# One block product fewer in each pair of layer A's projections, and attention operands read from two halves in turn

## The chip, the cores and the metric

The kernel runs on one core of a Trainium2 chip. The metric is the device time of one execution in microseconds (us), the median of three runs. A profile of one more execution shows where the time lies. TensorE is called PE here (its weight loads PEld), VectorE DVE, ScalarE ACT, GpSimd POOL, and SyncE, which issues most of the transfers, SP.

## What is computed

Two layers of a sequence model on 256 positions of width 2048, in float32. Layer A projects the normalised input to queries, keys, values and gates (4096 wide each, 32 heads of 128), attends in chunks with a learned bias by relative distance, multiplies by a gate and projects back to 2048. Layer B does the same with shared keys and values, a forget gate and a causal mask.

```python
# layer A
h = rms_norm(x, a_norm)
q, k, v, g = split(h @ a_w_in, 4)              # 2048 -> 4 x 4096
o = chunked_relbias_attention(q, k, v, a_rel_bias)
x = x + (o * silu(g)) @ a_w_out                # 4096 -> 2048
# layer B
k, v = split(rms_norm(x, kv_norm) @ kv_w, 2)
logf = log_sigmoid(rms_norm(x, kv_norm) @ f_w + f_b)
q, g = split(rms_norm(x, b_norm) @ b_w_in, 2)
o = forgetting_attention(q, k, v, cumsum(logf))
x = x + (o * silu(g)) @ b_w_out
return rms_norm(x, final_norm)
```

## The kernel before

**Products in three parts.** Float32 accuracy comes from splitting each operand into a high and a low part (`hi` by an ACT copy that rounds, `lo` by a DVE subtraction) and adding three products: hi times hi, hi times lo, lo times hi. `mm3` does this for the projections, `dot3` for the attention and the block products. The activations, split once, are the stationary operands (`xT`, `oA`, `x1T`, `oB`); the weights stream past.

**Units and sub-blocks.** A projection is cut into units of 512 output columns. A unit holds two accumulators of 128 positions by 512 columns (`acc[0]`, `acc[1]`) in PSUM. Layer A's input projection has 32 units: for each of the 16 head pairs g one for queries and keys (`aqk`) and one for values and gates (`avg`). A unit takes 8 sub-blocks; a sub-block is 256 rows of the weights (2 blocks of 128, 512 KB). It costs 12 matmuls of 128x512: 2 blocks, 2 halves of the positions, 3 parts.

**The feed.** `Feed` loads the sub-blocks on SP's queue in the order of one list, into 6 buffers (`raw`), and splits each into one of 4 buffers `hi` and `lo`. `get` hands the oldest to PE and splits ahead: while PE works on one sub-block, the third behind it is split, as soon as the buffer that PE has just left is free. The weights lie in two halves of each row (`IL` = 2), and `cols` reads them as the moving operand in turn, one element from the first half, one from the second, 2 KB apart.

**Attention beside it.** Each head pair's attention is a generator (`attention`, called by `side_a` and `side_b`) which is advanced between sub-blocks by tables (`PV_STEPS`, `QK_STEPS`, `OLD_A_STEPS`): a transposition of q and k (`turn`: one DVE pass, then 16 transfers, in layer A 12 issued by POOL and 4 by ACT), the split of k (`wideh`, `widel`) and q, the scores (`s1p`, `s0p`, in banks of the 4-bank pool `ps_at`), the softmax, a transposition of the probabilities (`sg`; 16 transfers by POOL), their split, the product with the values (`op`) and the gate (`oT`, `oA`). So the work of one pair lies beside the projections of the next. The scores and `op` take their moving operands, 256 positions, in one contiguous run.

**Block products.** In the output projections (`ao`, `bo`) some sub-blocks of two units are computed together by `Quad`: 2 halves of the positions, 2 blocks of rows and 2 units make a 2x2 by 2x2 product, done with 7 products of blocks where 8 would be plain: 21 matmuls of 128x512, not 24. DVE forms sums of the weights (`Quad.split`: four subtractions beside the splits), sums of the activations (`Quads.open`), and adds the partial results p1, p5, p7, p6, which fill all 4 banks of `ps_at`, into `comb` (one ACT copy, four DVE additions). The first quad's sub-blocks of both units come as two `raw` tiles, `one` and `two`; `Quad.split` subtracts the two halves of `two` ahead of anything else that it does.

**Order.** Each engine runs its instructions in the order in which they stand in its queue, and an instruction that waits holds all behind it. The order follows the code, where a scheduler may move an instruction that waits for nothing far ahead; `tc.issue_after(x)` keeps what is written under it behind instruction x.

## Time and profile before

| | |
|---|---|
| runs | 1755.29 us median (1753.59 to 1757.29) |
| profiled execution | 1757.04 us, its span 1755.3 us |
| granted PE clock | 0.998 |
| PE busy | 1738.7 us (99%), 8348 matmuls |
| DVE busy | 1243.2 us (71%) |
| ACT busy | 1107.2 us (63%) |
| POOL busy | 516.6 us (29%) |
| DMA | 396.35 MB, 226 GB/s |

The span runs from the first instruction of the profiled execution to the last; 1.7 us of the time lie around it. A row of the timeline gives start, duration, engine, line, operation and tiles; a square bracket at its end gives the idle time before it and what ended it. A row of a group gives after its shapes the count, then the busy time in us and the mean of one in ns, then idle time before. A PE row's duration is the whole passage of a matmul, about 380 ns, and matmuls overlap, so the cost of one is read from the distance of the starts. The table of windows gives the length of a window, then the busy time of each engine (instructions in brackets), the clock, the DMA engines' share and GB/s. Layer A's input projections take the span to about 710 us, `ao` to 873, layer B's projections to 1580, `bo` the rest. Names of engines with a q at the end (SPq) are their queues of transfers.

### The profile page before, as it was taken

How to read it: one execution, taken by the hardware profiler on the slowest of the kernel's cores; microseconds unless marked ns; L12 is line 12 of the kernel's file. 1: busy time of each engine (PE TensorE's matmuls, PEld its weight loads, DVE VectorE, ACT ScalarE, POOL GpSimd, SP SyncE). 2: the span in 40 equal slices, each digit the busy share in tenths (PEclk: the TensorE clock that was granted, in tenths of full speed). 3: DMA queues.
4: the chain of work that ended last, by engine and by line, in shares of the span. 5: the costliest groups of instructions: out<-in, count | busy, mean ns of one | idle time of the engine just before them, and what ended most of it. 6: DMA issues, size and time to landing. Idle time of an engine off the chain costs nothing.

```text
span 1755.3 us, 25640 instructions
## 1 busy us (share of the span) xinstructions
PE 1738.7 (99%) x8348; PEld 1527.7 (87%) x8348; DVE 1243.2 (71%) x1818; ACT 1107.2 (63%) x2103; POOL 516.6 (29%) x1071
## 2 busy tenths in 40 slices
PE   9999999999999999999999999999999999999997
PEld 7888888888888888888888888888888888888886
DVE  7666666666666686688966777777777777876687
ACT  6555555555555566556657777777777777665454
POOL 2333333333333333202103333333333333333000
PEclk9999999999999999999999999999999999999999
DMA  8776776776777677677767777777767777767654
GB/s 301 241 222 222 227 225 223 226 224 225 224 222 226 224 224 230 202 241 250 245 214 234 226 226 224 224 227 225 224 226 225 225 226 225 245 214 233 218 203 144
DMA packets 143654, 396.35 MB, mean 226 GB/s; under 512 B 31104, under 2 KB 38560, under 8 KB 143392
## 3 DMA queue, kind: packets, MB, share of 16 engines
q1 hardware_dynamic: 107472, 354.25, 62.9%
q0 software_dynamic: 32256, 37.29, 6.5%
q10 hardware_dynamic: 3792, 3.17, 0.6%
q8 instruction: 66, 1.08, 0.3%
q14 instruction: 68, 0.56, 0.1%
HBM read 351.05 MB, written 4.23 MB: 202 GB/s over the span
## 4 chain that ended last, share of the span: by engine, by line
PE 96%; DMA 1%; DVE 1%; ACT 0%; issue 0%; SPq 0%; POOL 0%; DVEq 0%; ACTq 0%
PE bkv_acc L184 19%; PE bqg_acc L184 19%; PE avg_acc L184 18%; PE aqk_acc L184 18%; PE bo_acc L184 8%; PE ao_acc L184 7%; PE op L575 1%; PE s0p L541 1%; PE p L519 0%; PE p L517 0%; PE p L518 0%; PE op L518 0%; PE s1p L518 0%; PE s1p L519 0%; PE s1p L517 0%; PE op L519 0%
## 5 line engine op out<-in xcount | busy, mean ns | idle before, releaser
L490 POOL DMA_DIRECT2D sgZ<-sgY x512 | 251.0, 497 | 193.8 <-DVE sgY L487 90.6
L490 POOL DMA_DIRECT2D turned<-turned x448 | 219.9, 498 | 265.3 <-PE avg_acc L184 94.7
L243 DVE SCALAR_TENSOR_TENSOR bqg_lo<-bqg_raw,gain,bqg_hi 128x512 fp32r<-128x512 f32 x256 | 182.6, 750 | 84.4 <-ACT bqg_hi L242 84.2
L242 ACT ACTIVATE bqg_hi<-bqg_raw,gain 128x512 fp32r<-128x512 f32 x256 | 170.7, 714 | 107.4 <-PE bqg_acc L184 51.8
L248 DVE TENSOR_TENSOR avg_lo<-avg_raw,avg_hi 128x1024 fp32r<-128x1024 f32 x127 | 153.3, 1219 | 109.6 <-ACT avg_hi L247 107.9
L248 DVE TENSOR_TENSOR aqk_lo<-aqk_raw,aqk_hi 128x1024 fp32r<-128x1024 f32 x125 | 152.4, 1219 | 86.8 <-ACT aqk_hi L247 85.4
L247 ACT ACTIVATE avg_hi<-avg_raw 128x1024 fp32r<-128x1024 f32 x127 | 132.4, 1055 | 121.2 <-PE aqk_acc L184 68.6
L243 DVE SCALAR_TENSOR_TENSOR bkv_lo<-bkv_raw,gain,bkv_hi 128x512 fp32r<-128x512 f32 x256 | 181.0, 748 | 38.3 <-ACT bkv_hi L242 35.6
L184 PE MATMUL bqg_acc<-bqg_hi,x1Th 128*128 128x512 f32 x512 | 192.2, 386 | 0.0
L184 PE MATMUL aqk_acc<-aqk_hi,xTh 128*128 128x512 f32 x512 | 190.4, 382 | 1.5 <-ACT aqk_hi L247 1.5
L184 PE MATMUL aqk_acc<-aqk_lo,xTh 128*128 128x512 f32 x512 | 189.1, 380 | 1.2 <-DVE aqk_lo L248 1.2
L184 PE MATMUL avg_acc<-avg_hi,xTh 128*128 128x512 f32 x512 | 190.2, 382 | 0.0
L184 PE MATMUL bqg_acc<-bqg_lo,x1Th 128*128 128x512 f32 x512 | 189.6, 381 | 0.0
L184 PE MATMUL bqg_acc<-bqg_hi,x1Tl 128*128 128x512 f32 x512 | 189.4, 380 | 0.0
L184 PE MATMUL bkv_acc<-bkv_hi,x1Th 128*128 128x512 f32 x512 | 189.1, 380 | 0.0
L247 ACT ACTIVATE aqk_hi<-aqk_raw 128x1024 fp32r<-128x1024 f32 x125 | 131.5, 1052 | 91.2 <-PE aqk_acc L184 43.5
L184 PE MATMUL bkv_acc<-bkv_lo,x1Th 128*128 128x512 f32 x512 | 188.9, 379 | 0.0
L184 PE MATMUL avg_acc<-avg_lo,xTh 128*128 128x512 f32 x512 | 188.9, 379 | 0.0
L184 PE MATMUL avg_acc<-avg_hi,xTl 128*128 128x512 f32 x512 | 188.9, 379 | 0.0
L184 PE MATMUL bkv_acc<-bkv_hi,x1Tl 128*128 128x512 f32 x512 | 188.9, 379 | 0.0
L184 PE MATMUL aqk_acc<-aqk_hi,xTl 128*128 128x512 f32 x512 | 188.9, 379 | 0.0
L242 ACT ACTIVATE bkv_hi<-bkv_raw,gain 128x512 fp32r<-128x512 f32 x256 | 168.7, 712 | 22.9 <-PE bqg_acc L184 16.5
(297 smaller groups left out, 3556.0 us busy)
## 6 DMA issues: line engine op xcount, KB each, us to landing
bqg_raw<-in_b_w_in SPq DMA_DIRECT2D x128, 512.0 KB, 4.3
bkv_raw<-in_kv_w SPq DMA_DIRECT2D x128, 512.0 KB, 4.0
avg_raw<-in_a_w_in SPq DMA_DIRECT2D x127, 512.0 KB, 4.2
aqk_raw<-in_a_w_in SPq DMA_DIRECT2D x125, 512.0 KB, 3.9
ao_raw<-in_a_w_out SPq DMA_DIRECT2D x64, 512.0 KB, 4.4
bo_raw<-in_b_w_out SPq DMA_DIRECT2D x64, 512.0 KB, 4.1
sgZ<-sgY POOLq DMA_DIRECT2D x512, 40.0 KB, 4.0
turned<-turned POOLq DMA_DIRECT2D x448, 32.0 KB, 3.7
```

The source lines that it names most:

```text
L184: pe.matmul(acc[t], x[:, t * P:(t + 1) * P], w, start=t not in begun, stop=last and i == 2)
L242: act.activation(hi[:, :, j], raw[:, :, j], AF.Copy, scale=gk)
L243: dve.scalar_tensor_tensor(lo[:, :, j], raw[:, :, j], gk, r32(hi[:, :, j]), op0=OP.mult, op1=OP.subtract)
L247: self.by_act = act.activation(hi[:, :, j], raw[:, :, j], AF.Copy)
L248: self.by_dve = dve.tensor_sub(lo[:, :, j], raw[:, :, j], r32(hi[:, :, j]))
L490: queues[j].dma_start(out=r32(z)[j * SQ:(j + 1) * SQ, i], in_=y[i * SQ:(i + 1) * SQ, j])
L541: pe.matmul(s0p[:, i], q0[:, i], qkT[:, HG + i, 0], start=True, stop=True)
L575: pe.matmul(op[:, i, P:], v1[:, i * DH:(i + 1) * DH], pT[:, i, NT], start=False, stop=i == HG - 1)
```

## The change

1. **A quad in each pair of layer A.** For g from 1 to 15, the last sub-block of `aqk` and that of `avg` (b = 7) become one quad, `a_pairs[g - 1]`. It is fed and run behind the fifth sub-block of the pair's first unit (`QUAD_STEP` = 5). It is a quad by itself, first and last, so its four products are combined at once into `comb`, an SBUF tile of its own. The query and key part of `comb` is scaled by ACT and added in the read-out of `aqk`, which moves from two ACT copies to two DVE operations; the value and gate part is added in `close_vg` by two DVE additions, and what follows reads SBUF and not PSUM. The activations' sums are formed once (`sum_up` after the first pair).
2. **Attention's steps** move to fit (`FIRST_STEPS`, `SECOND_STEPS`, `OLD_A_STEPS`): a pair's scores now stand behind the first sub-block of the next pair, the transposition of the probabilities behind the third, `op` behind the fourth sub-block of the next pair's second unit; the last pair's steps beside `ao` follow suit.
3. **Operands read in turn.** `split_pairs` writes hi and lo of an operand into one tile with its two halves of positions 2 KB apart, and the scores, `op` and the forget gate's `zp` read one position from each half in turn. The results come out interleaved, and the readers of `s1p`, `op` and `zp` in PSUM step over two elements; the two last products of `op` write every second column.
4. **Sums queued.** The sums in `Quads.open` are put behind the newest split on DVE (`tc.issue_after`).
5. The buffers of the first transposition (`home`) and of the start are laid into other tiles.

The diff, without the tile layout of the start:

```diff
-QK_STEPS = {0: 1, 6: 1, 7: 2}
-PV_STEPS = {1: 1}
-OLD_A_STEPS = {0: 1, 2: 99}
+QUAD_STEP = 5
+SECOND_STEPS = {0: 1, 6: 1}
+FIRST_STEPS = {0: 2, 2: 1}
+OLD_A_STEPS = {1: 1, 3: 99}
...
+                with tc.issue_after(feed.by_dve.ins):
+                    self.sum_up(lhs, b, two[:, b % 2], free)
...
+        def sum_up(self, lhs, b, dst, free):
+            self.sums[b] = dst
+            hi, lo = dst[:, 0], dst[:, 1]
+            xs, v = free[:, 0].rearrange("p (k s) -> p k s", s=S), free[:, 1].rearrange("p (i s) -> p i s", s=P)
+            k = b * KB
+            dve.tensor_add(xs, r32(lhs.hi[k // BIG][:, k % BIG:k % BIG + KB]),
+                           r32(lhs.lo[k // BIG][:, k % BIG:k % BIG + KB]))
+            a11, a21, a12, a22 = (xs[:, j, t * P:(t + 1) * P] for j in range(KB) for t in range(NT))
+            dve.tensor_add(v[:, 0], a21, a22)
+            dve.tensor_sub(v[:, 2], a11, a21)
+            dve.tensor_sub(v[:, 1], v[:, 0], a11)
+            dve.tensor_sub(v[:, 3], a12, v[:, 1])
+            act.activation(hi, v, AF.Copy)
+            dve.tensor_sub(lo, v, r32(hi))
...
+    a_quads = Quads("a", None)
+    a_pairs = [Quad(a_quads, qkvg[2 * g:2 * g + 2], KD // KB - 1, True, True) for g in range(1, NG)]
+    for quad in a_pairs:
+        first, second = (whole(sp_) for sp_ in quad.specs)
+        todo += first[:QUAD_STEP] + [(None, quad)] + first[QUAD_STEP:] + second
...
-            nt = srcs[0].shape[1]
-            out.append([att.tile([P, len(srcs), nt * P], F32R, name=f"{tag}{x}", tag=f"{tag}{x}") for x in "hl"])
+            out.append(att.tile([P, srcs[0].shape[1], 2, len(srcs), P], F32R, name=tag, tag=tag))
             if place is not None:
-                feed.behind(out[-1][0][:, :, :1], place)
+                feed.behind(out[-1][:, 0, 0, :, :1], place)
         for k in range(len(many[0][0])):
-            for (srcs, _), (hi, lo) in zip(many, out):
-                h, l = (v[:, k].rearrange("p (t i u) -> p t i u", t=srcs[k].shape[1], u=SQ) for v in (hi, lo))
+            for (srcs, _), both in zip(many, out):
+                h, l = (both[:, :, i, k].rearrange("p t (i u) -> p t i u", u=SQ) for i in range(2))
                 act.activation(h, srcs[k], AF.Copy)
                 dve.tensor_sub(l, srcs[k], r32(h))
-        return out
+        return [[both[:, :, i].rearrange("p t k n -> p k n t") for i in range(2)] for both in out]
...
-            dot3(s1p[:, i], (qh[:, i], ql[:, i]), (kh[:, i], kl[:, i]))
+            dot3(s1p[:, i], (qh[:, i, :, 0], ql[:, i, :, 0]), (kh[:, i], kl[:, i]))
...
-            dve.scalar_tensor_tensor(s_, sp_, SCALE, bias, op0=OP.mult, op1=OP.add)
+            if t:
+                for i in range(HG):
+                    to, plus = (v[:, i].rearrange("p (t n) -> p t n", t=NT) for v in (s_, bias))
+                    dve.scalar_tensor_tensor(to, sp_[:, i].rearrange("p (n t) -> p t n", t=NT), SCALE, plus,
+                                             op0=OP.mult, op1=OP.add)
+            else:
+                dve.scalar_tensor_tensor(s_, sp_, SCALE, bias, op0=OP.mult, op1=OP.add)
...
-            pe.matmul(op[:, i, P:], v1[:, i * DH:(i + 1) * DH], pT[:, i, NT], start=False, stop=i == HG - 1)
+            pe.matmul(op[:, i, 1::NT], v1[:, i * DH:(i + 1) * DH], pT[:, i, NT], start=False, stop=i == HG - 1)
...
-            dve.tensor_mul(*(v[:, i].rearrange("p (t i u) -> p t i u", t=NT, u=SQ) for v in (oT, op)), gT[:, i])
+            dve.tensor_mul(oT[:, i].rearrange("p (t i u) -> p t i u", t=NT, u=SQ),
+                           op[:, i].rearrange("p (i u t) -> p t i u", t=NT, u=SQ), gT[:, i])
...
+        if g:
+            for t in range(NT):
+                dve.scalar_tensor_tensor(qk[:, t], accs["qk"][t], rsA[:, t:t + 1], a_quads.comb[:, t],
+                                         op0=OP.mult, op1=OP.add)
+        else:
+            evac_scaled(accs["qk"], 0, UN, rsA, qk)
...
-    def close_vg(accs):
+    def close_vg(accs, g):
+        if g:
+            for t in range(NT):
+                whole_ = a_quads.comb[:, NT + t]
+                dve.tensor_add(whole_, accs["vg"][t], whole_)
+                accs["vg"][t] = whole_
...
-            accs["qk"] = drive(unit(xT), prev, PV_STEPS)
-            vg = unit(xT)
+            first, second = (Unit(xT, next(order)) for _ in range(2))
+            def products():
+                a_pairs[g - 1].step(xT, first, second)
+                for t in range(NT):
+                    act.activation(a_quads.comb[:, t], a_quads.comb[:, t], AF.Copy, scale=rsA[:, t:t + 1])
+            accs["qk"] = drive(rest(first), prev, FIRST_STEPS, {QUAD_STEP - 1: products})
+            vg = rest(second)
         else:
             first, second = woven_units()
             rsA, halfA = rs
             accs["qk"], vg = first.acc, rest(second)
         old, prev = prev, side_a(g, accs)
         advance(prev)
-        accs["vg"] = drive(vg, prev, QK_STEPS, {}, old, OLD_A_STEPS)
-        close_vg(accs)
+        accs["vg"] = list(drive(vg, prev, SECOND_STEPS, {}, old, OLD_A_STEPS))
+        if not g:
+            a_quads.sum_up(xT, KD // KB - 1, sums[:, 0], a_quads.comb)
+        close_vg(accs, g)
...
-    project(oA, ao, ao_order, ao_begun, ao_closed, [(prev, [2, 6, 2, 1]), (ao_quads.open(oA, QUADS), [3, 1, 1, 2, 2])])
+    project(oA, ao, ao_order, ao_begun, ao_closed, [(prev, [1, 0, 2, 6, 2, 1]), (ao_quads.open(oA, QUADS), [3, 1, 1, 2, 2])])
...
-            pe.matmul(zp, both, x1T.h(k), start=k == 0, stop=False)
-            pe.matmul(zp, both, x1T.l(k), start=False, stop=k == KD - 1)
+            hi, lo = (v.rearrange("p (t n) -> p n t", t=NT) for v in (x1T.h(k), x1T.l(k)))
+            pe.matmul(zp, both, hi, start=k == 0, stop=False)
+            pe.matmul(zp, both, lo, start=False, stop=k == KD - 1)
...
```

**PE, a quad of layer A.** Before, the sub-block behind the fifth of an `aqk` unit is plain (hi and lo are the weights' parts, xTh and xTl those of the activations):

```order
L184 MATMUL aqk_acc_1420<-aqk_hi_1484,xTh_106 128x512
L184 MATMUL aqk_acc_1420<-aqk_lo_1485,xTh_106 128x512
L184 MATMUL aqk_acc_1420<-aqk_hi_1484,xTl_108 128x512
L184 MATMUL aqk_acc_1421<-aqk_hi_1484,xTh_106 128x512
L184 MATMUL aqk_acc_1421<-aqk_lo_1485,xTh_106 128x512
L184 MATMUL aqk_acc_1421<-aqk_hi_1484,xTl_108 128x512
```

Now the quad stands there (`p` are the partial products in PSUM, `sums` the activations' sums); its first two steps:

```order
L528 MATMUL p_1588<-quad_hi_1510,xTh_106 128x512
L529 MATMUL p_1588<-quad_lo_1511,xTh_106 128x512
L530 MATMUL p_1588<-quad_hi_1510,xTl_108 128x512
L528 MATMUL aqk_acc_1445<-quad_hi_1510,xTh_106 128x512
L529 MATMUL aqk_acc_1445<-quad_lo_1511,xTh_106 128x512
L530 MATMUL aqk_acc_1445<-quad_hi_1510,xTl_108 128x512
L528 MATMUL p_1589<-quad_hi_1554,sums 128x512
L529 MATMUL p_1589<-quad_lo_1555,sums 128x512
L530 MATMUL p_1589<-quad_hi_1554,sums 128x512
L528 MATMUL p_1590<-quad_hi_1554,sums 128x512
L529 MATMUL p_1590<-quad_lo_1555,sums 128x512
L530 MATMUL p_1590<-quad_hi_1554,sums 128x512
```

The 12 matmuls of the two units' last sub-blocks are gone, 24 in each pair, and 21 stand here; the list of PE is 45 matmuls shorter.

**DVE, ahead of a pair's scores.** Before, the end of a pair's second unit (`aqk_lo` are splits for the next pair, `widel` and `q1l` belong to the scores' operands):

```order
L248 TENSOR_TENSOR avg_lo_1712<-avg_raw_1560,avg_hi_1711 128x1024
L248 TENSOR_TENSOR aqk_lo_1730<-aqk_raw_1578,aqk_hi_1729 128x1024
L248 TENSOR_TENSOR aqk_lo_1748<-aqk_raw_1604,aqk_hi_1747 128x1024
L510 TENSOR_TENSOR widel<-turned,wideh 128x256
L510 TENSOR_TENSOR q1l<-turned,q1h 128x128
L510 TENSOR_TENSOR widel<-turned,wideh 128x256
L510 TENSOR_TENSOR q1l<-turned,q1h 128x128
L248 TENSOR_TENSOR aqk_lo_1783<-aqk_raw_1647,aqk_hi_1782 128x1024
L594 SCALAR_TENSOR_TENSOR vl<-avg_acc_1598,rstd_a,vh 128x256
L548 SCALAR_TENSOR_TENSOR sg<-s1p,tb 128x2x256
```

Now, at the same place (the transposed q and k, `turned` before, lie in the tile `sums`; `first_102` holds the quad's sums of weights):

```order
L249 TENSOR_TENSOR aqk_lo_1815<-aqk_raw_1666,aqk_hi_1814 128x1024
L290 TENSOR_TENSOR first_102<-avg_raw_1770 128x2x256
L249 TENSOR_TENSOR aqk_lo_1833<-aqk_raw_1690,aqk_hi_1832 128x1024
L521 TENSOR_TENSOR wide<-sums,wide 128x2x128
L521 TENSOR_TENSOR q_1852<-sums,q_1852 128x128
L521 TENSOR_TENSOR wide<-sums,wide 128x2x128
L521 TENSOR_TENSOR q_1852<-sums,q_1852 128x128
L720 TENSOR_TENSOR comb<-avg_acc_1447,comb 128x512
L720 TENSOR_TENSOR comb<-avg_acc_1448,comb 128x512
L612 SCALAR_TENSOR_TENSOR vl<-comb,rstd_a,vh 128x256
L624 SCALAR_TENSOR_TENSOR gs<-gs,comb 128x256
L249 TENSOR_TENSOR aqk_lo_1883<-aqk_raw_1726,aqk_hi_1882 128x1024
```

The quad's first subtraction (L290, which needs the tile `two`, here avg_raw_1770, from memory) stands between two splits and ahead of the scores' operands; two additions to `comb` follow these.

**DVE, the quad.** Before, from the transposition of the probabilities on, there are only splits:

```order
L248 TENSOR_TENSOR aqk_lo_1441<-aqk_raw_1285,aqk_hi_1440 128x1024
L487 STREAM_TRANSPOSE sgY<-sg 128x1280
L248 TENSOR_TENSOR aqk_lo_1485<-aqk_raw_1303,aqk_hi_1484 128x1024
L248 TENSOR_TENSOR aqk_lo_1503<-aqk_raw_1321,aqk_hi_1502 128x1024
L248 TENSOR_TENSOR aqk_lo_1521<-aqk_raw_1339,aqk_hi_1520 128x1024
L248 TENSOR_TENSOR avg_lo_1539<-avg_raw_1374,avg_hi_1538 128x1024
```

Now the quad's subtractions and splits stand around it:

```order
L249 TENSOR_TENSOR aqk_lo_1490<-aqk_raw_1317,aqk_hi_1489 128x1024
L289 TENSOR_TENSOR first_102<-avg_raw_1337,aqk_raw_1335 128x2x256
L574 RECIPROCAL csc<-sm 128x4
L575 TENSOR_TENSOR csc<-csc,half_a 128x4
L296 TENSOR_TENSOR quad_lo_1511<-aqk_raw_1335,quad_hi_1510 128x1024
L499 STREAM_TRANSPOSE sgY<-sg 128x1280
L298 TENSOR_TENSOR aqk_raw_1335<-avg_raw_1337,first_102 128x2x256
L296 TENSOR_TENSOR quad_lo_1555<-first_102,quad_hi_1554 128x1024
L299 TENSOR_TENSOR aqk_raw_1335<-aqk_raw_1335 128x2x256
L296 TENSOR_TENSOR quad_lo_1571<-avg_raw_1337,quad_hi_1570 128x2x256
L296 TENSOR_TENSOR quad_lo_1593<-aqk_raw_1335,quad_hi_1592 128x1024
L249 TENSOR_TENSOR aqk_lo_1605<-aqk_raw_1385,aqk_hi_1604 128x1024
```

Behind these come splits with the four additions to `comb` and the two read-outs of `aqk` between them.

More of the change, by code (lines that the diff above doesn't have):

```diff
@@ L387, in whole, with spec @@
+    def spec(name, w, nk, late=0, kept=0, g0=None, quads=0):
+        return dict(name=name, w=w, nk=nk, late=late, kept=kept, g0=g0, plain=nk // KB - quads)
     def whole(spec):
[L388 removed]
+        return [(spec, b) for b in range(spec["plain"])]
     qkvg = []
     for g in range(NG):
[L392 to L393 removed]
+        qkvg.append(spec(f"aqk{g}", a_w_in[2 * g], KD, quads=g > 0))
+        qkvg.append(spec(f"avg{g}", a_w_in[2 * g + 1], KD, quads=g > 0))
@@ L443, in rest @@
     def rest(u):
-        for b in range(u.nk // KB - u.left, u.nk // KB):
+        for b in range(u.done, u.plain):
             u.step(b)
@@ L611, in trunk @@
     feed.early += [first[i][:, j] for i in range(2) for j in range(2)]
-    sq = [big_tile([P, BIG, S], F32, name="sq0"), first[1].rearrange("p r a j n -> p (r a j) n")]
-    turned = big_tile([P, 2, NQ, 2 * HG * NT, SQ], F32, name="turned")
-    home = [turned[:, i] for i in range(2)]
+    a_quads.t, a_quads.comb = first[1], big_tile([P, 2 * NT, UN], F32, name="comb")
+    sums = big_tile([P, 2, 2, 4, P], F32R, name="sums")
+    home = [v.rearrange("p (i c u) -> p i c u", i=NQ, u=SQ) for v in
+            (first[1][:, 1].rearrange("p a j n -> p (a j n)"), sums[:, 1].rearrange("p a k s -> p (a k s)"))]
+    sq = [a_quads.comb.rearrange("p a (k s) -> p (a k) s", s=S), first[1].rearrange("p r a j n -> p (r a j) n")]
     xT = Stat("xT", KD)
-    xr, homes = {}, iter(["wideh", "tb", "widel", "oT", "gs", "R", "Y", "Z", "wideh"])
+    xr, homes = {}, iter(["wide", "tb", None, "oT", "gs", "R", "Y", "Z", "wide"])
     def load_xT(k0, k1):
-        xr[k0] = att.tile([P, k1 - k0, S], F32, name=f"xr{k0}", tag=next(homes))
+        home_ = next(homes)
+        if home_ is None:
+            xr[k0] = xr["wide"][:, 1]
+        else:
+            both = att.tile([P, 1 + (home_ == "wide"), KB, S], F32, name=f"xr{k0}", tag=home_)
+            xr[k0], xr[home_] = both[:, 0, :k1 - k0], both
         sp.dma_start(out=xr[k0], in_=x_t[:, k0:k1])
```

36 lines of the change are left out of this document (9 added, 27 removed).

## The prediction

> **What bounds the kernel now.** I read the page first, then PE's waits, the chain of waits, the windows and the timelines of PE, DVE and ACT in one pair of layer A. Three rows of the page: the span, PE, and the chain by engine.
>
> ```profile
> span 1755.3 us, 25640 instructions
> ...
> PE 1738.7 (99%) x8348; PEld 1527.7 (87%) x8348; DVE 1243.2 (71%) x1818; ACT 1107.2 (63%) x2103; POOL 516.6 (29%) x1071
> ...
> PE 96%; DMA 1%; DVE 1%; ACT 0%; issue 0%; SPq 0%; POOL 0%; DVEq 0%; ACTq 0%
> ```
>
> PE is busy for all but 16.6 us, and 96% of the chain that ended last is PE's own work. PE's waits on other engines (in all, times, longest):
>
> ```profile
> PE op L517 <- ACT wideh L509: 2.0, 2, 1.4
> ...
> PE aqk_acc L184 <- ACT aqk_hi L247: 1.5, 1, 1.5
> ...
> PE heat L110 <- DVE zeros L107: 1.3, 1, 1.3
> ...
> PE aqk_acc L184 <- DVE aqk_lo L248: 1.2, 2, 0.9
> ...
> PE ao_acc L184 <- DVE ao_lo L248: 0.5, 1, 0.5
> ```
>
> They come to a few us, at the start and at single places. So time can be won only by giving PE fewer or shorter matmuls; work on DVE and ACT counts only where PE comes to wait for it. The chain's pieces give the cost of a matmul and the length of a pair:
>
> ```profile
> 360.49 20.72 PE aqk_acc L184 x96
> ...
> 404.26 20.72 PE aqk_acc L184 x96
> ```
>
> 96 matmuls of 128x512 in 20.72 us are 0.2158 us each; a pair of layer A takes 404.26 - 360.49 = 43.77 us. A pair, the start of `ao`, and the stretch with all of `ao`'s quads, in the table of windows:
>
> ```profile
> 324.00:367.77 43.77, 43.77 (x214) 38.64 (x213) 28.22 (x37) 25.85 (x46) 13.90 (x29) 1.00 0.72 226
> 710.67:745.00 34.33, 34.33 (x166) 30.22 (x165) 23.51 (x31) 17.60 (x31) 8.88 (x19) 1.00 0.64 203
> 740.00:873.00 133.00, 132.54 (x614) 115.50 (x613) 115.42 (x143) 78.31 (x110) 18.89 (x39) 1.00 0.71 237
> ```
>
> In a pair PE has no idle time, DVE works 28.2 us, ACT 25.9.
>
> **The change part by part: the quads.** Each quad puts 21 matmuls of 128x512 where 24 were, and the list of PE is 45 shorter: 15 pairs x 3 x 0.2158 = 9.7 us off the bounding engine. Some of these matmuls start a product in a bank of its own; `ao` does the same at 0.22 us each in the chain, so the price holds.
>
> **Operands in turn.** Columns show the start of six matmuls of 256 positions (scores), four of 128, the next projection; then the first of 32 of `zp` and what follows them:
>
> ```profile
> 315.39 0.28 PE L517 MATMUL s1p<-wideh,q1h 128*128 128x256 f32 x1
> ...
> 316.11 0.61 PE L541 MATMUL s0p<-turned,q 128*128 128x128 f32 x4
> ...
> 316.47 0.68 PE L184 MATMUL aqk_acc<-aqk_hi,xTh 128*128 128x512 f32 x2
> ...
> 897.36 0.28 PE L799 MATMUL zp<-x1Th,fwp 128*64 128x256 f32 x1
> ...
> 901.00 0.38 PE L184 MATMUL bkv_acc<-bkv_hi,x1Th 128*128 128x512 f32 x1
> ```
>
> Six contiguous reads of 256 take 316.11 - 315.39 = 0.72 us, 0.120 each; `zp`, with 64 columns of weights, (901.00 - 897.36)/32 = 0.114. The projections, which already read two halves in turn, 2 KB apart as the new tile is, take 0.2158 for 512, that is 0.108 for 256. So the contiguous read costs 6 to 12 ns more, and more with more weights. Bounds for 12 such matmuls in each of 32 pairs (scores and `op`, both layers): nothing, if weight loads and not the read set the 0.120, to 384 x 0.012 = 4.6 us. The row of four 128-wide matmuls shows how fast weights can change: 316.47 - 316.11 = 0.36, and the matmul behind starts its successor some 0.08 late, so about 0.11 each. I take 0.111: 384 x 0.009 = 3.5 us; `zp` gives 32 x 0.003 = 0.1. [...]
>
> **What DVE and ACT get for it.** Groups with count, busy time, mean ns:
>
> ```profile
> L248 DVE TENSOR_TENSOR aqk_lo<-aqk_raw,aqk_hi 128x1024 fp32r<-128x1024 f32 x125 | 152.4, 1219 | 86.8 <-ACT aqk_hi L247 85.4 <-DMA aqk_raw<-in_a_w_in 1.4
> ...
> L288 DVE TENSOR_TENSOR ao_quad<-ao_raw,ao_raw 128x512 f32<-128x512 f32 x8 | 5.6, 695 | 0.0
> ...
> L295 DVE TENSOR_TENSOR quad_lo<-ao_raw,quad_hi 128x512 fp32r<-128x512 f32 x8 | 5.5, 683 | 0.9 <-ACT quad_hi L294 0.9
> ...
> L338 DVE TENSOR_TENSOR ao_quad<-ao_quad,p 128x512 f32<-128x512 f32 x2 | 1.4, 678 | 0.0
> ...
> L548 DVE SCALAR_TENSOR_TENSOR sg<-s1p,tb 128x512 f32<-128x512 f32 x16 | 11.1, 691 | 4.8 <-PE s1p L519 4.7
> ...
> L548 DVE SCALAR_TENSOR_TENSOR sg<-s0p,tb 128x256 f32<-128x256 f32 x16 | 6.6, 413 | 0.0
> ...
> L496 ACT ACTIVATE qk<-aqk_acc,rstd_a 128x512 f32<-128x512 f32 x32 | 21.3, 687 | 15.1 <-PE aqk_acc L184 13.2 <-POOL rstd_a L124 1.9
> ...
> L294 ACT ACTIVATE quad_hi<-ao_raw 128x512 fp32r<-128x512 f32 x8 | 5.0, 630 | 8.3 <-PE ao_acc L184 8.2
> ...
> L337 ACT ACTIVATE ao_quad<-p 128x512 f32<-128x512 f32 x2 | 1.2, 579 | 0.0
> ```
>
> Per pair DVE gets: four subtractions of 512 (4 x 0.69), splits of 1024 three times and of 512 once in place of two of 1024 (1.22 + 0.68), four additions to `comb` (2.71), two read-outs (1.4) and two additions in `close_vg` (1.4), and the scores' 512 become two of 256 (0.13): 10.3 us, so 38.5 of 43. ACT gets one split of 1024 and one of 512 (1.7), a copy of p1 (0.58) and two scalings (1.3), and loses two read-outs (1.37): 2.2, so 28 of 43. Neither reaches PE's time. The precedent is `ao`: there DVE worked 115.4 of 133 us (87%) with 8 quads, and PE lacked 133.00 - 132.54 = 0.46. 15 quads at that rate are 0.9 us, which I book as loss (none to 15 x 0.3).
>
> The readers of `s1p` and `op` step over two elements in PSUM. No row shows that on DVE; a 512 takes 691 ns and a 256 413, so 1.09 per element, and doubled that is 0.28 more for each of four instructions, half of them ahead of the quad. That lies inside the slack worked out next, so nothing on PE.
>
> **The tight place** is ahead of the scores. DVE now meets the quad's first subtraction between two splits, and this must wait for the tile `two` from memory; behind it stand one split, the operands of the scores and everything after. ACT's split, the DVE splits (the one before, and its own), the last of the scores' operands, and the scores on PE:
>
> ```profile
> 354.23 1.06 ACT L247 ACTIVATE aqk_hi<-aqk_raw 128x1024 fp32r<-128x1024 f32 x1 [1.53 <-PE avg_acc L184]
> ...
> 352.73 1.23 DVE L248 TENSOR_TENSOR aqk_lo<-aqk_raw,aqk_hi 128x1024 fp32r<-128x1024 f32 x1 [1.42 <-ACT aqk_hi L247]
> ...
> 355.32 1.23 DVE L248 TENSOR_TENSOR aqk_lo<-aqk_raw,aqk_hi 128x1024 fp32r<-128x1024 f32 x1 [1.36 <-ACT aqk_hi L247]
> ...
> 357.33 0.28 DVE L510 TENSOR_TENSOR q1l<-turned,q1h 128x128 fp32r<-128x128 f32 x1
> ...
> 359.16 0.28 PE L517 MATMUL s1p<-wideh,q1h 128*128 128x256 f32 x1
> ```
>
> DVE idles 1.36 us ahead of this split, since ACT can only start when PE frees a buffer. The subtraction takes 0.61 of these (512 back to back), so a wait of 0.75 is free. The operands end at 357.61, the scores start at 359.16: 1.55 to spare. The new order keeps the two sub-blocks between that split and the scores, so up to 2.3 us of waiting cost PE nothing. Now the wait: `two` takes the sixth buffer back, freed by the split two ahead of it in DVE's list; between these lie one sub-block and `op` on PE, 2.6 + 1.1 = 3.7 us. Time to landing, in layer A's pairs and then in `ao`, and the one time that this subtraction waited long:
>
> ```profile
> L206 SPq DMA_DIRECT2D aqk_raw<-in_a_w_in x104: 327/328/328, 118.4 to 663.0; - x104
> ...
> DMA to landing us min/median/max: 3.0/3.7/6.0
> ...
> DMA to landing us min/median/max: 3.2/4.4/7.8
> ...
> 732.18 0.69 DVE L289 TENSOR_TENSOR ao_quad<-ao_raw 128x512 f32<-128x512 f32 x1 [3.62 <-DMA ao_raw<-in_a_w_out]
> ```
>
> At the median of 3.7 the wait is nearly nothing, at the longest of layer A, 6.0, it is 2.3, just free; at `ao`'s 7.8 it is 4.1 and stalls PE 1.8. Median it is: no loss. Further back the quad's splits: they follow PE's buffers, with 1.5 us or so to spare by the same durations, and POOL's transfers of the transposed q and k, which the new order brings closer to their readers, eat of the same 1.55 if they come late.
>
> **First pair, and `ao`.** PE's waits between 60 and 110 us:
>
> ```profile
> PE op L517 <- ACT wideh L509: 0.6, 1, 0.6
> PE op L518 <- DVE widel L510: 0.6, 1, 0.6
> ```
>
> Here the first pair's split, transfers and `op` came in one step, out of phase; now the first pair follows the other tables, and `op` comes 2 sub-blocks after its split. 1.2 us off (0 to 1.2). The sums of `ao`, in each of five sub-blocks:
>
> ```profile
> L371 DVE TENSOR_TENSOR ao_quad<-oAh,oAl 128x512 f32<-128x512 f32 x5 | 3.4, 686 | 0.1
> ...
> L374 DVE TENSOR_TENSOR ao_quad<-ao_quad 128x128 f32<-128x128 f32 x5 | 1.4, 285 | 0.1
> ```
>
> With the split of each (0.69) they are 5 x (0.69 + 4 x 0.285 + 0.69) = 12.6 us of DVE, some 10 back to back. They ran in layer A's last pairs and are now held behind splits at the start of `ao`, where DVE has 23.5 of 34.3: full. By the splits' lead over PE I put the cost at 0 to 2, an estimate. The longest wait of the list above, 1.4 for `op`'s operands, lies near 1539 in layer B's last pairs, where the sums for `bo` ran, and may go. I take 0 for both.
>
> **Sum:** 9.7 + 3.5 + 0.1 + 1.2 - 0.9 = 13.6 off the profiled span of 1755.3. That execution took 1757.04, 1.75 over the median of the runs; as the terms are differences, I set them against the median: 1755.3 - 13.6 = 1741.7.
>
> **Rivals.** *1. Pairs stall in part.* A late `two`, late transfers and slow PSUM reads add up past the slack, and PE lacks 0.3 to 0.9 us in each pair: 5 to 13 of the gain return, 1746 to 1751. For it: DVE at 90% in strict order; against: `ao`. *2. Slower.* `two` lands late in every pair: the subtraction heads DVE's queue, the scores' operands behind it come late and PE stands. It decides where the stall passes 13.6/15 = 0.9 us, a landing of 6.9; at 7.8, 1.8 x 15 = 27: 1769. For it: 732.18 waited 3.62 in just this manner. Against: there the DMA engines were also moving x and probabilities, and 104 transfers of layer A never took over 6.0. *3. PSUM writes with a step.* The last products of `op`, 4 of 128 in a pair, write every second column. If one then takes as long as a 512, 0.2158 and not 0.111, 128 x 0.105 = 13.4 us return: 1755, no change. For half speed, 128 columns in the time of 256, 0.108, the weights still hide it. [...] *4. The reads don't speed up:* 1745, inside my range.
>
> **Chances.** As summed, with or without the reads' part, 1738 to 1746: 0.68. Rival 1: 0.13. Rival 2: 0.09. Rival 3: 0.06. Something that no row shows: 0.04. Measurements of this kernel can tell 0.2%, 3.5 us, from no change. Faster takes the first two, 0.81; same 0.09 (rival 3 and a part of the rest), slower 0.10. The range 1738 to 1751 holds the first two cases; its low end has the reads at 4.6, no loss in the quads and the 1.4 near 1539 gone.
>
> **What would show it.** A pair of layer A of 43.0 us in the chain (43.77 - 0.65 - 0.11) and one of layer B shorter by 0.1; six scores in 0.67; no wait of PE in the pairs, DVE near 38 us in each; the subtraction waiting under 1 us for its transfer; no wait of `op` at 80 us. Wrong would be rows of PE waiting for `widel`'s successor, `wide`, or for `quad_lo` in most pairs, scores still at 0.72, or `op`'s last products further apart than 0.11.

## The result and the profile after

The changed kernel takes 1743.86 us (median of 6, 1743.65 to 1746.91), the kernel before 1754.47 beside it (6 runs, 1753.59 to 1757.29). The ratio is 0.9943, 95% interval 0.9932 to 0.9953; the medians differ by 10.6 us. The forecast was 1741.7 in a range of 1738 to 1751. The profiled execution took 1746.91, the slowest of the six, so its stalls are on the large side.

The page after: span, PE, and the chain by engine.

```profile
span 1745.2 us, 25902 instructions
...
PE 1725.5 (99%) x8303; PEld 1513.7 (87%) x8303; DVE 1375.6 (79%) x2066; ACT 1140.9 (65%) x2164; POOL 517.0 (30%) x1071
...
PE 91%; DVE 4%; DMA 3%; ACT 1%; issue 1%; SPq 0%; ACTq 0%; DVEq 0%
```

PE's work went down by 13.2 us (1738.7 to 1725.5), about as much as the sum had for quads and reads together (13.3), but the span only by 10.1. The agreement is in part chance: of PE's busy time before, about 1.7 us is a stretch at half clock near 1540, which is told below and has nothing to do with the number of matmuls. The chain, 96% PE before, is 91% PE with 4% DVE and 3% DMA in it: some waits are new. PE's waits (in all, times, longest):

```profile
PE ao_acc L185 <- DVE ao_lo L249: 4.7, 3, 1.7
...
PE aqk_acc L185 <- ACT aqk_hi L248: 1.4, 2, 0.9
...
PE bo_acc L529 <- DVE quad_lo L296: 1.2, 1, 1.2
...
PE ao_acc L529 <- DVE quad_lo L296: 0.8, 1, 0.8
```

None lies in a pair of layer A or B. `op`, which headed the list before, is gone from it; new is `ao_lo`, 4.7 us at three places, all in `ao`. The chain of waits gives the length of a pair: two starts of the same piece in layer A, two in layer B, and then two of layer B in the kernel before.

```profile
352.95 2.59 PE aqk_acc L185 x12
...
395.98 2.59 PE aqk_acc L185 x12
...
1109.15 2.59 PE bqg_acc L185 x12
...
1152.83 2.59 PE bqg_acc L185 x12
```

```profile
1117.54 20.72 PE bkv_acc L184 x96
...
1161.29 20.72 PE bkv_acc L184 x96
```

A pair of layer A takes 395.98 - 352.95 = 43.03 us (43.0 was forecast), one of layer B 1152.83 - 1109.15 = 43.68, 0.07 or 0.08 less than the 43.75 of before (1161.29 - 1117.54). The windows of one pair and of `ao`'s quads, columns as before:

```profile
352.95:395.98 43.03, 43.03 (x211) 37.96 (x210) 36.99 (x52) 28.02 (x51) 13.89 (x29) 1.00 0.70 229
...
740.00:868.00 128.00, 123.27 (x567) 107.03 (x568) 109.43 (x134) 71.93 (x104) 19.23 (x40) 1.00 0.70 238
```

In the pair PE has no idle time, and DVE works 37.0 of 43 us (38.5 was forecast). In `ao`'s quads PE lacks 128.00 - 123.27 = 4.7 us, where before it lacked 0.46 in 133.

The first of the six scores and of the four products behind them, the last operand of the scores on DVE, and `op`'s last four products (they write every second column) with the matmul after them:

```profile
355.38 0.27 PE L528 MATMUL s1p<-wide,q 128*128 128x256 f32 x1
...
356.05 0.61 PE L552 MATMUL s0p<-sums,q 128*128 128x128 f32 x4
```

```profile
353.55 0.28 DVE L521 TENSOR_TENSOR q<-sums,q 128x128 fp32r<-128x128 f32 x1
```

```profile
387.59 0.61 PE L592 MATMUL op<-sgZ,v 128*128 128x128 f32 x4
...
387.96 0.46 PE L185 MATMUL avg_acc<-avg_hi,xTh 128*128 128x512 f32 x1
```

Six scores take 356.05 - 355.38 = 0.67 us as forecast, 0.72 before. `op`'s last four take 387.96 - 387.59 = 0.37, as the four contiguous ones did: writing PSUM with a step costs nothing that shows here. The operands are ready at 353.83, 1.55 ahead of the scores, the very number worked out beforehand.

The subtraction that waits for the tile `two`, in layer A and in `ao`: its instructions, what ended its waits, and the landing times of layer A's transfers.

```profile
L290 DVE TENSOR_TENSOR first<-avg_raw x15: 691/692/694, 51.2 to 652.3; 128x512 f32<-128x512 f32 x15
...
L290 DVE TENSOR_TENSOR ao_quad<-ao_raw x8: 684/692/693, 720.9 to 838.2; 128x512 f32<-128x512 f32 x8
...
  DMA avg_raw<-in_a_w_in: 9.4, 13
...
  DMA ao_raw<-in_a_w_out: 9.3, 6
```

```profile
DMA to landing us min/median/max: 3.1/4.5/7.5
```

In layer A the wait is 9.4 us over 13 pairs, 0.7 each, though the transfers got slower (median 4.5 and longest 7.5, from 3.7 and 6.0). In `ao` it is 9.3 over 6.

Where the time went is seen by lining up the scores of the 32 pairs in the two profiles. Up to the last scores of layer A the kernel gains 12.4 us; here 2.6 is allowed for, since these scores now come one sub-block later in the list. From there to layer B's first scores it loses 6.8. In layer B it gains 4.9, of which 3.8 in one place: before, one pair took 47.55 us, with PE's 1.36 us wait near 1538 in it, and the window behind that wait shows about half the granted clock:

```profile
1540.29:1543.70 3.41, 3.41 (x10) 2.72 (x10) 3.41 (x7) 2.35 (x5) 2.93 (x6) 0.50 0.58 172
```

These 3.41 us at a clock of 0.50 do the work of 1.7. This pair is now 43.68 like the others. The end loses 0.35. So -12.4 + 6.8 - 4.9 + 0.4 = -10.1.

### The profile page after: what moved, and what is told of

Its sections match the earlier page's. It is cut to its first block, busy times and chain, and to the rows that moved or that the text cites. A ratio compares the mean times of both kernels' runs of the same rounds, so it can differ in the third digit from the quotient of the medians.

```text
span 1745.2 us, 25902 instructions
## 1 busy us (share of the span) xinstructions
PE 1725.5 (99%) x8303; PEld 1513.7 (87%) x8303; DVE 1375.6 (79%) x2066; ACT 1140.9 (65%) x2164; POOL 517.0 (30%) x1071
## 4 chain that ended last, share of the span: by engine, by line
PE 91%; DVE 4%; DMA 3%; ACT 1%; issue 1%; SPq 0%; ACTq 0%; DVEq 0%
PE bkv_acc L185 19%; PE bqg_acc L185 19%; PE aqk_acc L185 16%; PE avg_acc L185 16%; PE bo_acc L185 8%; PE ao_acc L185 3%; DMA ao_raw<-in_a_w_out 2%; DVE ao_lo L249 1%; PE p L530 1%; PE p L529 1%; PE p L528 1%; DVE quad_lo L296 1%; PE s0p L552 1%; PE op L592 1%; PE s1p L530 0%
## 5 line engine op out<-in xcount | busy, mean ns | idle before, releaser
L502 POOL DMA_DIRECT2D sums<-first x448 | 219.9, 498 | 324.6 <-DVE wide L521 147.6
L185 PE MATMUL aqk_acc<-aqk_hi,xTh 128*128 128x512 f32 x452 | 167.6, 382 | 1.4 <-ACT aqk_hi L248 1.4
L185 PE MATMUL avg_acc<-avg_hi,xTh 128*128 128x512 f32 x452 | 167.5, 382 | 0.2 <-ACT avg_hi L248 0.2
L185 PE MATMUL aqk_acc<-aqk_lo,xTh 128*128 128x512 f32 x452 | 166.3, 379 | 1.0 <-DVE aqk_lo L249 1.0
L185 PE MATMUL aqk_acc<-aqk_hi,xTl 128*128 128x512 f32 x452 | 166.1, 379 | 0.0
L185 PE MATMUL avg_acc<-avg_hi,xTl 128*128 128x512 f32 x452 | 166.1, 379 | 0.0
L185 PE MATMUL avg_acc<-avg_lo,xTh 128*128 128x512 f32 x452 | 166.1, 379 | 0.0
L248 ACT ACTIVATE avg_hi<-avg_raw 128x1024 fp32r<-128x1024 f32 x112 | 116.1, 1050 | 75.9 <-PE avg_acc L185 50.3
L249 DVE TENSOR_TENSOR avg_lo<-avg_raw,avg_hi 128x1024 fp32r<-128x1024 f32 x112 | 136.4, 1219 | 31.4 <-ACT avg_hi L248 31.4
L249 DVE TENSOR_TENSOR aqk_lo<-aqk_raw,aqk_hi 128x1024 fp32r<-128x1024 f32 x110 | 134.0, 1222 | 25.4 <-ACT aqk_hi L248 20.3
```

The source lines that it names most:

```text
L185: pe.matmul(acc[t], x[:, t * P:(t + 1) * P], w, start=t not in begun, stop=last and i == 2)
L248: self.by_act = act.activation(hi[:, :, j], raw[:, :, j], AF.Copy)
L249: self.by_dve = dve.tensor_sub(lo[:, :, j], raw[:, :, j], r32(hi[:, :, j]))
L502: queues[j].dma_start(out=r32(z)[j * SQ:(j + 1) * SQ, i], in_=y[i * SQ:(i + 1) * SQ, j])
```

## The experiments

Two theories on the 6.8 us in `ao` were set against each other. S: the five sums, held back to `ao`'s start, fill DVE and eat up the lead of the splits over PE. D: DVE waits at the head of its queue for a transfer, the tile `two`. (In the first expectation D still stands for transfers that came late by chance.) The medians of before, run beside the four sets, lay between 1754.08 and 1755.12.

**The changed kernel again.**

> The changed kernel once more, as the base of the others and for a second profile. Theory S (sums): the start of ao, where all five sums of the quads now crowd VectorE, loses PE's lead, and PE then stands some 5 to 8 us in ao; the median is 1743.9 give or take 1.5, and the profile shows PE's waits in ao of at least 4 us again, pairs of layer A at 43.03 and of layer B at 43.67. Rival D (transfers): the waits come from transfers of ao_raw that land late in this one execution; then the waits in ao lie elsewhere or are under 2 us, and the pairs are the same.

1744.36 us. The pairs take 43.03 and 43.67, but for one stall of 1.2 us in a pair near 550. PE's waits in `ao`:

```profile
PE ao_acc L185 <- DVE ao_lo L249: 2.8, 3, 1.3
...
PE ao_acc L529 <- DVE quad_lo L296: 0.8, 1, 0.8
```

3.6 us in all, at the same places as in the first profile: the loss is the program's own, its size varies. S had expected at least 4 and D under 2 or other places, so chance is out, and the list doesn't decide between S and a wait for `two` that recurs.

**Where the sums are.** Three edits: the sums not held behind the split; the sums of `ao` further apart; only one sum.

```diff
-                with tc.issue_after(feed.by_dve.ins):
-                    self.sum_up(lhs, b, two[:, b % 2], free)
+                self.sum_up(lhs, b, two[:, b % 2], free)
```

> The sums of ao and bo are no longer held behind the feed's last split: in program order two of ao's then stand in layer A's last pairs, three in ao, and bo's five in layer B's last pairs as before the change. Theory S: ao's waits fall from some 7 us to about 4, the two pairs of layer A with a sum (2.5 us more on 37 of 43) stay at 43.0 or lose under 1 us each, and layer B's last pairs lose 1.5 to 4 us again, as before the change (47.55 us for one pair); in all 1742 to 1747. Rival D: ao as it was, layer B 1.5 to 4 us longer: 1745.5 to 1748.

```diff
-(ao_quads.open(oA, QUADS), [3, 1, 1, 2, 2])
+(ao_quads.open(oA, QUADS), [4, 3, 3, 18, 3])
```

> The sums of ao are computed at the 4th, 7th, 10th, 28th and 31st sub-block of ao, not all within the first nine: each only needs to be there before its quad. Theory S: VectorE has 5 us less to do in the first 40 us of ao, keeps its lead, and PE's waits in ao fall from some 7 us to under 3: 1738 to 1741. Rival D: the waits stay, since they are for transfers: 1743 to 1745.

```diff
-                    self.sum_up(lhs, b, two[:, b % 2], free)
+                    if b and self.name == "ao":
+                        self.sums[b] = self.sums[0]
+                    else:
+                        self.sum_up(lhs, b, two[:, b % 2], free)
```

> Of ao's five sums only the first is computed, and all five quads read that one: 4 x 2.5 us of VectorE and four ACT copies of 0.63 us are left out. Theory S: PE's waits in ao nearly go, to under 1.5 us: 1736.5 to 1739.5. Rival D: the subtraction still waits for the tile `two` at the head of VectorE's queue, and PE waits some 1.5 us at three or four places: 1742 to 1744.

1745.84, 1745.74 and 1743.15 us: S expected 3 us of gain or more from the second and third; against 1744.36 they lost 1.4 and gained 1.2. PE's waits for `ao_lo` in the three, in this order, and then DVE's first subtraction of `two` in the kernel with one sum:

```profile
PE ao_acc L185 <- DVE ao_lo L249: 3.2, 2, 2.4
```

```profile
PE ao_acc L185 <- DVE ao_lo L249: 3.4, 3, 2.0
```

```profile
PE ao_acc L185 <- DVE ao_lo L249: 2.9, 2, 2.2
```

```profile
722.13 0.69 DVE L290 TENSOR_TENSOR ao_quad<-ao_raw 128x512 f32<-128x512 f32 x1 [4.04 <-DMA ao_raw<-in_a_w_out]
```

By the waits S alone is out: with one sum it expected under 1.5 us, and PE still waits 2.9 there. The medians alone would say less, since each of these three profiles holds a stretch of 3.41 us at half clock, some 1.7 us lost, and the two of the changed kernel hold none. The wait of the subtraction is 4.04 us, where with all sums it was 2.16 (at 720.91). DVE doesn't come earlier for having less to do: in both it begins to wait 19.2 us behind layer A's last scores. The tile lands later, and why is not shown. Not held back, `ao`'s sums are done from 689.2 to 717.7 in place of 712.2 to 731.8, and layer A's pairs keep 43.03 but for one of 43.96. `bo`'s first sum is begun at 1489.4 (1497.2 before the change), but its last step comes only at 1557.9 (1508.7 before), and layer B's pairs keep 43.67: the expected loss in layer B did not come. That the new layout of the memory holds this step back is a guess, not shown.

**The wait at the head of the queue.** The second subtraction needs only `two`, and so had been placed 9 us ahead of the first. Now it is tied behind the same split.

```diff
-                feed.behind(t[:, :, 0, :1], -1)
+                feed.behind(t[:, :, 0, :1], -1); feed.behind(t[:, :, 1, :1], -1)
```

> The quad's second subtraction, which needs only the tile `two`, stood some 9 us ahead of the first on VectorE, where it waited for that tile's transfer at the head of the queue: 0.7 us in each pair of layer A and 1 to 4 us in ao. It is tied behind the same split as the first one, and stands next to it. Theory D (this wait at the head of the queue costs ao its lead): the waits go in layer A, and in ao PE's waits fall from 3.6 to 7 us to under 2: 1740 to 1742.5, with the pairs of layer A still at 43.03. Rival: the lead is set by VectorE's load, which is the same: 1743.5 to 1745. If the two subtractions in a row make the quad's splits late, PE waits for quad_lo in each pair, and the time rises above 1747.

1741.07 us, 3.3 less than the changed kernel; ratio to before 0.9920 (0.9906 to 0.9933). The longest waits of PE, and the window of `ao`'s quads:

```profile
PE heat L111 <- DVE zeros L108: 1.3, 1, 1.3
...
PE aqk_acc L185 <- ACT aqk_hi L248: 0.9, 1, 0.9
...
PE bo_acc L529 <- DVE quad_lo L296: 0.7, 1, 0.7
...
PE ao_acc L529 <- DVE quad_lo L296: 0.7, 1, 0.7
```

```profile
740.00:862.00 122.00, 122.00 (x567) 106.68 (x566) 108.50 (x134) 72.88 (x111) 20.15 (x42) 1.00 0.74 249
```

The subtraction waits for no transfer any more, PE has no idle time in these 122 us, with the same quads and sums, and `ao_lo` is off the list. From the last scores of layer A to the first of layer B it takes 226.55 us; with the 2.6 for the moved scores that is as long as before the change (229.26). This is D, shown by taking the wait away: without it there is no loss.

The wait alone is not the whole cause, though, for the kernel before had it too. There the same subtraction waited 5.9 us in `ao`, over five times, with the 3.62 that the prediction shows among them, and PE lacked 0.46; in the second profile after the change it waited 6.0 over six, and PE waited 3.6. So the change must also have taken away what made up for the wait. The hold on the sums does a part (alone it makes `ao` 1.4 us longer, see below), the quads of layer A another (without them `ao` loses 2.8 by the same reckoning, not 4.1 to 6.8). The rest is open. With both edits at once:

> Both edits that concern ao at once: the second subtraction behind the same split as the first, and the sums at the 4th, 7th, 10th, 28th and 31st sub-block. Theory D (the transfer that VectorE waits for at the head of its queue is the whole of ao's loss): with that wait gone the sums cost nothing wherever they stand, and the time is that of the tied subtraction alone, 1740 to 1742. Rival S (the sums cost lead as well): 1738 to 1739.5, with no wait of PE in ao at all.

1740.70 us (0.9924, 0.9912 to 0.9937): the same within the scatter of the runs (1737.52 to 1741.57 and 1739.86 to 1741.07). Once the wait is gone, no effect of the place of the sums shows. Either of the two is the best version here.

**One part at a time.** First without layer A's quads (specs, list of sub-blocks and read-outs as for the first pair):

```diff
-    qkvg.append(spec(f"aqk{g}", a_w_in[2 * g], KD, quads=g > 0))
+    qkvg.append(spec(f"aqk{g}", a_w_in[2 * g], KD))
...
-                a_pairs[g - 1].step(xT, first, second)
```

> The changed kernel without its 15 quads in layer A: all else, the order of steps, the alternate reads and the place of the sums in ao, stays. Theory Q (the quads are free): pairs of layer A take 43.03 + 0.65 = 43.67, and ao loses as much as with the quads: 1744.4 + 9.7 = 1754, 1752.5 to 1755.5. Rival L (the quads cost ao its lead, since VectorE has 37 of 43 us in a pair): PE's waits in ao fall under 2 us and the time is 1749 to 1752.

1751.86 us, 7.5 more than with them. Two pieces of its chain, and PE's wait in `ao`:

```profile
313.22 2.59 PE aqk_acc L185 x12
...
356.89 2.59 PE aqk_acc L185 x12
```

```profile
PE ao_acc L185 <- DVE ao_lo L249: 2.0, 2, 1.3
```

The pairs are 356.89 - 313.22 = 43.67, the 0.65 that three matmuls make; but 9.7 was to be had and 7.5 came. `ao` is 1.3 us shorter without the quads (from the last scores of layer A to the first of layer B 229.50, with them 230.76 in the second profile and 233.51 in the first), and the stall near 550 is absent. So both expectations were half right. Then the operands laid out contiguously, with `op`'s results and the readers in PSUM as they were before:

```diff
-out.append(att.tile([P, srcs[0].shape[1], 2, len(srcs), P], F32R, ...
+out.append(att.tile([P, 2, len(srcs), srcs[0].shape[1], P], F32R, ...
```

> The changed kernel with the operands of the scores and of op laid out contiguously again, and op's results and their readers too; zp stays alternate. Theory R (each 256-wide matmul reads 8 ns faster in turn): pairs of layer A take 43.12, of layer B 43.75, six scores 0.72 us, in all 16 x 0.1 + 16 x 0.08 = 2.9 us more: 1746.5 to 1748.5. Rival: the gain per pair came with the moved steps, and the time stays within 0.7 us of 1744.4.

1747.20 us, 2.8 more. The first score and the products behind the six:

```profile
355.97 0.28 PE L528 MATMUL s1p<-wide,q 128*128 128x256 f32 x1
...
356.68 0.61 PE L552 MATMUL s0p<-sums,q 128*128 128x128 f32 x4
```

0.71 us for six, not 0.67; the six of `op` take 0.72, not 0.66; pairs 43.11 and 43.75. The gain is the reads'. Quads 7.5 and reads 2.8 make 10.3, each uncertain by about 1 us by the scatter of the runs; of the 10.6 us nearly nothing is left for everything else in the change (steps, hold, layout), whose gains and losses about cancel.

**The kernel before, again and with the hold alone.**

> The kernel before once more, for a second profile. In the first one a pair of layer B took 47.55 us instead of 43.75: PE waited 1.36 us for the operands of op near 1538 and then ran at a granted clock of 0.54 for 3.7 us. Theory P (the order of the work sets it): the same pair is 45 us or longer again, and the span is near 1755. Rival C (one late transfer by chance): all pairs of layer B take 43.75, and the span is 3 to 4 us shorter, 1751 to 1752. In both cases PE stands under 1.5 us in ao, the pairs of layer A take 43.77, and the first op waits 1.2 us in two pieces near 81.

Its `op` in layer B waits 1.60 us this time, at the same place, and the pair takes 47.59:

```profile
1538.09 0.38 PE L517 MATMUL op<-wideh,vh 128*128 128x256 f32 x1 [1.60 <-ACT wideh L509]
```

The order sets it. With the hold alone (`with tc.issue_after(feed.by_dve.ins):` around the sums):

> The kernel before with one part of the change alone: the sums of ao and bo are held behind the feed's last split when they are issued, so that they run in ao and bo and not in the last pairs of layers A and B. Theory B (bo's sums, at 1507 to 1520, pushed the transfers of the probabilities back by 4 us, and PE stood and then ran at half clock near 1538): all pairs of layer B take 43.75, 3.8 us less; in ao, where VectorE then has 10 us more to do, PE's waits grow from 0.5 to between 1 and 5 us; in all 1750 to 1753. Rival: the 47.6 us pair has another cause and stays, and with ao's loss the time is 1755 to 1759.

```profile
1494.00:1554.00 60.00, 60.00 (x299) 53.11 (x298) 42.66 (x73) 41.80 (x91) 22.45 (x47) 1.00 0.75 244
```

```profile
PE ao_acc L184 <- DVE ao_lo L248: 1.1, 2, 0.6
```

In the profile the stall goes with the sums, as theory B has it: no idle time and a full clock over the whole stretch where it was, and pairs of 43.75. That it came by way of the transfers of the probabilities is not shown. In `ao` there are 1.1 us of waits for `ao_lo`, and from the last scores of layer A to the first of layer B it takes 230.63 us, 1.4 more than before. But the median is 1753.80 against 1754.08, ratio 1.0000 (0.9991 to 1.0009), above the range expected. The runs lie within 2 us, those of before within 6. Both profiled executions of before, 1757.04 and 1756.46, were among its slower ones, so the stall may be there in a part of the executions only; this stays open.

**How thick the cover is.** The subtraction that waits for `two` is done three and nine times over in layer A's quads:

```diff
-dve.tensor_sub(t[:, :, 1], two[:, :, 1], two[:, :, 0])
+[dve.tensor_sub(t[:, :, 1], two[:, :, 1], two[:, :, 0]) for _ in range(3 if self.all is a_quads else 1)]
```

> In each pair of layer A the subtraction that waits for the tile `two` is done three times over: 1.2 us more of VectorE ahead of the scores' operands, back to back. In the changed kernel these operands are ready 1.55 us before PE starts the scores, and VectorE idles 0.95 us between here and the quad's last splits, which PE uses 0.95 and 0.8 us after they end. Theory K (the quads' work is free because it lies inside this cover): pairs stay at 43.03, and the time is 1744 to 1746. Rival (VectorE's order is already tight): each pair gets longer by 0.5 us or more, 1752 or above.

> The same subtraction nine times over: 1.2 us more ahead of the scores' operands as in the other, and some 3.7 us more between the quad's subtractions and its second split, where the cover is 0.95 us. VectorE then has 42 of 43 us in a pair. Theory K: the cover is used up, PE waits 2 to 3.5 us for quad_lo in each of 15 pairs and, after waits of 2 us and more, runs some matmuls at half the granted clock, 1.5 us more: 1775 to 1820. Rival (what VectorE has to do in a pair counts, not where): 42 of 43 fit, and the time stays under 1755.

1755.88 and 1808.98 us. PE's waits, of the one with two matmuls of a quad, and of the other with a window of one pair:

```profile
PE aqk_acc L529 <- DVE quad_lo L296: 1.8, 9, 0.2
```

```profile
155.90 0.38 PE L528 MATMUL aqk_acc<-quad_hi,xTh 128*128 128x512 f32 x1
...
156.49 0.48 PE L529 MATMUL aqk_acc<-quad_lo,xTh 128*128 128x512 f32 x1 [0.20 <-DVE quad_lo L296]
```

```profile
PE p L528 <- ACT quad_hi L295: 26.1, 15, 2.0
...
PE aqk_acc L528 <- ACT quad_hi L295: 6.0, 13, 0.5
```

```profile
165.45:168.81 3.36, 3.36 (x10) 2.69 (x9) 3.19 (x4) 2.60 (x4) 3.36 (x7) 0.51 0.83 224
```

With three, pairs take 43.7 on average. The list shows only 0.2 us for nine of them, but the matmul that waits starts 156.49 - 155.90 = 0.59 us after the one ahead of it in place of 0.22, and the next one is 0.1 late. The rival was right: 1.2 us more on DVE, in a pair where it idles for 6, costs 11.5 us, more than the quads had gained. With nine, PE waits 26.1 + 6.0 us, and in 12 of 15 pairs some ten matmuls behind the wait run at half the clock (0.51 in this window); such pairs take 47.3 to 48.1 us. That theory K held here, where the cover is used up, says little; the other run shows how little cover there was.

## Why the forecast held, and where it did not

- Quads, 9.7: right in the pairs (43.03, no wait in the first profile), by matmuls not done. The 0.9 booked for stalls was booked in the wrong place: the first profile has none in layer A, the second one stall of 1.2; the other loss is in `ao`. Net 7.5.
- Alternate reads, 3.5 and 0.1: 2.8. The row that they were taken from was right (0.67 for six scores); 0.08 in a pair of either layer (43.11 to 43.03, 43.75 to 43.67) over 12 matmuls is 7 ns each, not 9. `zp` comes to 0.109 each now, the scores to 0.112.
- `op`'s PSUM writes with a step: 0.37 for four, so rival 3 is out. A slowing to half speed, 0.108 each by the prediction's estimate, would lie under the 0.11 that each of the four takes in both kernels (0.37, and the 0.08 by which the matmul behind them is late), so that much isn't excluded.
- `two` in layer A: the wait of under 1 us came as worked out, and so did the 1.55 us ahead of the scores. But "up to 2.3 us of waiting cost PE nothing" is wrong: 1.2 more already cost 0.7 a pair. The sentence looked at the scores alone; the same lateness goes on to the quad's last splits, and these end 0.95 us before PE needs them.
- The first `op`: its wait is gone, as forecast. It had cost about 1.8, not 1.2, as two rows of before show: the second matmul starts 1.02 us after the first, 0.9 late; the first starts 1.02 after the projection's last matmul (80.26), 0.8 late, and the third another 0.1.

```profile
81.28 0.39 PE L517 MATMUL op<-wideh,vh 128*128 128x256 f32 x1 [0.64 <-ACT wideh L509]
...
82.30 0.39 PE L518 MATMUL op<-widel,vh 128*128 128x256 f32 x1 [0.64 <-DVE widel L510]
```

- `ao`, priced at 0 within 0 to 2: this is the step that failed. Measured 6.8 in one profile, 4.1 in the other by the same reckoning. The row that explains it stood in the prediction, 732.18 with 3.62 us of waiting for `two`; I used it for layer A alone, and in `ao` I counted DVE's work, not what it waits for. The row by itself would not have given the loss either, since in the kernel before it cost PE next to nothing; what was missing is how much lead DVE would still have behind it.
- The 1.4 near 1539, priced at 0: 3.8 in the profile. About 2.1 of it are the late matmuls of `op`, 1.7 the half clock behind them.

The last two have opposite signs, so the total came nearer than its parts, and that is luck: -9.7 - 2.8 - 1.8 + 6.8 - 3.8, with 0.6 lost at the start (what is left over up to the second pair) and 0.4 at the end, make -10.3 where the spans differ by 10.1.

## What to carry to other kernels

An instruction that waited for a transfer held back everything behind it in its queue (before the change DVE's subtraction waited 3.62 us up to 732.18, and the split behind it, whose `ao_hi` ACT had done at 729.90, began at 732.79), and that cost time where the engine had no lead left to make it up (in `ao`, 5.9 us of such waits cost 0.5 before the change, 6.0 cost 3.6 after it); a scheduler that puts it early because its operands allow that puts the wait early too. Tie such an instruction behind the work that must not wait, before looking for less work: here one more tie gave 3.3 us, and leaving out four of five sums 1.2. And measure a cover by adding work to it: a mean of 6 idle us in a pair was worth less than 1.2 at the place where it counted.

## What the runs showed of the hardware

After some of PE's waits the granted clock is 0.50 for 3.41 us, the same length in all 17 places, with eight matmuls of 128x512 at 0.43 us each. That is 1.7 us lost on top of the wait, where PE would not have had to wait again. It began 0.2 to 2.0 us after waits of 2.0, 2.2 and 2.4 us in `ao` (sums apart, one sum, sums not held), after 1.36 and 1.60 in layer B before the change, and in 12 of the 15 pairs with nine subtractions. In the first profile after the change it did not come after single waits of 1.38, 1.63 and 1.68.

The length of the wait doesn't decide this alone. In the run with nine subtractions the waits of 1.80 and 0.47 us in the first two rows were followed by such a stretch, from 165.32 to 168.73; the longer ones of the last two rows, 1.86 and 0.46, were not:

```profile
163.37 0.70 PE L528 MATMUL p<-quad_hi,sums 128*128 128x512 f32 x2 [1.80 <-ACT quad_hi L295]
...
164.84 0.48 PE L528 MATMUL aqk_acc<-quad_hi,xTh 128*128 128x512 f32 x1 [0.47 <-ACT quad_hi L295]
...
353.39 0.70 PE L528 MATMUL p<-quad_hi,sums 128*128 128x512 f32 x2 [1.86 <-ACT quad_hi L295]
...
354.86 0.48 PE L528 MATMUL aqk_acc<-quad_hi,xTh 128*128 128x512 f32 x1 [0.46 <-ACT quad_hi L295]
```

What differs is where they fall. The slow stretches of this run begin at 69.75, 117.54, 165.32, 213.11, 260.90, 400.84 us and so on; all twelve lie whole multiples of 3.413 us apart (14, 41 or 27 of them), though the pairs vary from 45.3 to 48.1 us. So in this run the stretches begin on a grid of that step, which the pairs' lengths do not shift. Ahead of 165.32, one step of the grid holds 1.46 and 0.47 us of the waits, 1.93 in all. The wait that ends at 353.39 is cut by a point of the grid at 353.05: one step holds 1.53 of it, the next 0.33 and the 0.46. An estimate from the starts, at 0.2158 us for 512 columns: in each of the 17 steps just ahead of a slow stretch, over all profiles, PE had matmuls for 0.65 to 1.28 us of the 3.41, and in every other step between the first scores and the last quad for 1.29 or more. The estimate also tells 1.36 us in layer B, where the step holds the short matmuls of `op` and the gaps between them (1.1 us of work), from 1.68 in `ao` (1.5). By it the limit lies near 0.38 of a step in these profiles; the two nearest cases, 0.375 and 0.379, are closer together than the estimate is sure. One of the windows, with one sum:

```profile
741.39:744.75 3.36, 3.36 (x10) 2.61 (x8) 3.33 (x5) 0.00 (x0) 0.00 (x0) 0.51 0.83 250
```
